# Two column groups of the embedding's gate as a seven-product pair, with sums of the third norm's activation

## The chip, the cores and the metric

The kernel runs on one core of a Trainium2 chip. A core has a matrix engine (TensorE, PE in the profile; PEld is its weight load), VectorE (DVE), ScalarE (ACT), GpSimd (POOL) and SyncE (SP), which issues most of the DMA transfers. Each engine works through its own queue in order and waits for the others by semaphores. The metric is the device time of one execution in microseconds; lower is better.

## The reference, cut to what matters

One layer on 256 rows of 2048 channels in float32: a feed-forward part, a mixer, a second feed-forward part, each with a layer norm behind it, and last the per-layer embedding, which is what the change touches:

```python
x = _layer_norm(ALPHA * x + 0.5 * _swiglu(x, ffn2_w1[i], ffn2_w3[i], ffn2_w2[i]), ln3_g[i], ln3_b[i])
x = x + jax.nn.sigmoid(x @ w_ple_gate[i]) * (p[i] @ w_ple_proj[i])
```

The gate is a product of 256x2048 by 2048x2048, the projection one of 256x256 by 256x2048. `_layer_norm` here is the third norm.

## The kernel before, in words

**Products.** Every float32 product is made of three matmuls in a rounded float32 format (fp32r in the profile): operand a is held as a high part and a low part, and hi x hi, hi x lo and lo x hi are summed (lines 1319 to 1321). A weight tile (`raw`) has 256 rows by 512 columns, seen as 128 partitions x 1024. It is split once: ScalarE casts the high part (L1264), VectorE subtracts it for the low part (L1268). An activation is held transposed in `ActT` tiles, high and low part alike, one for each chunk of 512 channels and each half of 128 rows. A `Unit` is one weight tile against one row half: 6 matmuls of 128x512.

**Groups.** `group` makes the plain product for 512 columns: 8 weight tiles, each used by two units, one for each row half (t = 0, 1). When a row half is complete, `done` reads the sum from PSUM.

**Seven products.** `seven` computes two column groups together by a Strassen-like scheme: over 4 chunks i of 512 channels it makes 7 units M1, M5, M7, M6, M3 and later M4, M2, where 8 plain units would stand for the same block. It needs sums of weights: M6 and M4 are made by VectorE (`plus`, L366); M5 and M7 either by VectorE or, where the chunk is in `loaded`, by a load that GpSimd issues and that adds to what is in the tile (`plus_load`, L372). It also needs sums of the activation, the `forms`: `form_turn` (L305) makes four sums of 128x256 on VectorE (L310 to L314) from the whole, unsplit activation (`act.whole`) and then splits them (L287 on ScalarE, L288 on VectorE). `both7` turns the seven products into two column groups (its `done`: copies on ScalarE, sums on VectorE, L420 and L426). `in_line` lays the units of such pairs in line, `weave` mixes them evenly into the plain units, by columns. The feed-forward parts and the mixer run this way; the embedding did not.

**Order.** The whole order is written out while the program is built. `program` is a list of units; a walk over it emits each unit's matmuls, then runs the work that is due (`Sched`, a clock in estimated microseconds with a heap of delayed turns), then emits further splits and loads. `HELD` limits by mode how many raw tiles and split pairs may be held at once; in the mode that rules the embedding before, (11, 6). `PAGES` is the pool of 51 pages that raw tiles, splits, activations and residuals share. `DELAY["form"]` and 5.0 set when the form turn of a chunk is due. What is emitted is fixed: at run time each engine follows its queue.

**The norm and the end.** `Norm.finish` normalizes, `Norm.turn` transposes a chunk (L519), applies scale and shift on ScalarE (L243, four 128x128 pieces), and splits (L287, L288); `Norm.affine` (L546, L547) later does the same to the residual on VectorE, two operations of 128x512 for each row half and chunk. The third norm turned its activation into tiles without forms. Then come four groups of the projection (L1168 copies them out) and four groups of the gate. `ple_done` takes a sigmoid (L243), multiplies by the projection (L1180), adds the residual (L1181) and stores (L1182). The last two tiles of the last group are `skewed`: both tiles for row half 0, then both for row half 1, and that group is finished in halves of 256 columns.

Of the kernel before, what the change touches and what calls it, by code (L numbers as in the profile page):

```python
# [10 lines left out]
ACT = mybir.ActivationFunctionType  # L11
ALU = mybir.AluOpType

P = 128
S = 256
TT = S // P
D = 2048
# [6 lines left out]
COL = 512  # L24
# [2 lines left out]
TEMP_BUFS = 6  # L27


HELD = {"ffn": (11, 6), "mix": (6, 6), "woven": (9, 6), "wide": (11, 6)}  # L30
RAW_EDGE, SPLIT_EDGE = 4, 11
EDGE = 6

AHEAD = 3
PSUM_BUFS = 8
SKEW = 6

HEAD = 20

# [15 lines left out]
DELAY = {  # L55
    "alpha": 24.0, "away": 5.0, "sig": 5.0, "form": 18.0, "ln_turn": 3.6, "ln_step": 2.1, "gb": 14.0, "h": 8.0, "silu": 6.0, "late": 9.0, "last": 5.0, "rest": 1.2, "mt": 3.2,
    "sbt": 4.6, "g0": 3.0, "g1": 4.0, "g2": 12.0, "cv0": 1.0, "cv1": 5.0, "cv2": 1.3,
    "m0": 4.0, "m1": 4.0, "m2": 2.0, "m3": 4.6, "m4": 4.6, "sa": 1.4, "s0": 6.5, "s1": 8.5, "s2": 3.0, "s3": 5.0, "s4": 5.5,
}
# [47 lines left out]
class ActT:  # L107


    def __init__(self, alloc, forms=None, later=False):  # L110
        self.alloc, self.soon = alloc, forms is not None and not later
        self.forms, self.whole = forms, {}
        self.tiles = {}
        self.left = {}

    def get(self, c, tt):
        if (c, tt) not in self.tiles:
# [48 lines left out]
def weave(main, side):  # L166

    n = sum(u.cols for u in main if isinstance(u, Unit))
    out, at, seen = [], 0, 0
    for u in main:  # L170
        out.append(u)
        if isinstance(u, Unit):
            seen += u.cols
            while at < len(side) and at * n < seen * len(side):
                out.append(side[at])
                at += 1
    return out
# [11 lines left out]
def kernel(  # L189
# [6 lines left out]
    nc = tc.nc  # L196
# [15 lines left out]
    def temp():  # L212
        sched.until(lambda: temps[0] < TEMP_BUFS)
        temps[0] += 1
        return temp_pool.tile([P, COL], F32, name="temp", tag="temp")

    def drop(n=1):
        temps[0] -= n
# [22 lines left out]
    def activate(out, in_, func, **kw):  # L241
        use_table(func)
        nc.scalar.activation(out, in_, func, **kw)  # L243
# [13 lines left out]
    def xres(t, c0, n=COL):  # L257
        return res[t, c0 // 1024][:, c0 % 1024:c0 % 1024 + n]
# [31 lines left out]
    def transposed(src, act, c, t):  # L290
        ps = misc([P, 4, P])
        for k in range(4):
            nc.tensor.transpose(ps[:, k], src[:, k * P:(k + 1) * P], ident[:])  # L293
        dst = act.get(c, t)
        nc.scalar.copy(dst[:, 0], ps[:])  # L295
        if act.soon:
            if c not in act.whole:
                act.whole[c] = big()
            nc.scalar.copy(act.whole[c][:, t * COL:(t + 1) * COL], ps.rearrange("q k s -> q (k s)"))  # L299
        nc.vector.tensor_tensor(out=dst[:, 1], in0=ps[:], in1=dst[:, 0], op=ALU.subtract)  # L300
        act.mark(c, t, 4)
        if act.soon and all(act.ready(c, h) for h in range(TT)):
            sched.spawn(form_turn(act, c), DELAY["form"] + 5.0 * c)

    def form_turn(act, c):  # L305

        a = [act.whole[c][:, t * COL:(t + 1) * COL] for t in range(TT)]
        s12, s34 = temp(), temp()
        l, r = slice(0, 2 * P), slice(2 * P, 4 * P)
        nc.vector.tensor_tensor(out=s12[:, l], in0=a[1][:, r], in1=a[1][:, l], op=ALU.subtract)  # L310
        nc.vector.scalar_tensor_tensor(out=s12[:, r], in0=s12[:, l], scalar=-1.0, in1=a[0][:, l],  # L311
                                       op0=ALU.mult, op1=ALU.subtract)
        nc.vector.tensor_tensor(out=s34[:, l], in0=a[0][:, l], in1=a[1][:, l], op=ALU.subtract)
        nc.vector.tensor_tensor(out=s34[:, r], in0=a[0][:, r], in1=s12[:, r], op=ALU.add)  # L314
        yield 4.0
        for h, src in enumerate((s12, s34)):
            dst = act.forms.get(c, h)
            split_psum(dst[:, 0], dst[:, 1], src.rearrange("q (k s) -> q k s", s=P))
            drop()
            act.forms.mark(c, h, 4)  # L320
# [18 lines left out]
    def group(w, rows, col0, cols, act, done):  # L339

        accs = [{} for _ in range(TT)]
        pairs = []
        for i, r in enumerate(rows):
            tile = plain(rows_of(w, r, col0, cols))
            pairs.append([Unit(tile, t, accs[t], act, r // COL, r % COL // P,
                               i == 0, i == len(rows) - 1, done) for t in range(TT)])
        return pairs
# [110 lines left out]
    def mode(name):  # L458
        program.append(Mode(name))
# [6 lines left out]
    class Norm:  # L466
# [33 lines left out]
        def finish(self, t):  # L500
            mv = small.tile([P, 2], F32, name="mv", tag="mv")
            nc.vector.bn_aggr(out=mv[:], in_=self.stats[t][:])  # L502
            rstd = small.tile([P, 1], F32, name="rstd", tag="rstd")
            activate(rstd[:], mv[:, 1:2], ACT.Sqrt, bias=eps[:, 0:1])
            nc.vector.reciprocal(out=rstd[:], in_=rstd[:])
            for c in range(4):
                xs = xres(t, c * COL)
                nc.vector.tensor_scalar(out=xs, in0=xs, scalar1=mv[:, 0:1], scalar2=rstd[:, 0:1],
                                        op0=ALU.subtract, op1=ALU.mult)
                sched.spawn(self.turn(t, c), DELAY["ln_turn"] + DELAY["ln_step"] * c)  # L510
            return
            yield

        def turn(self, t, c):

            xs, act = xres(t, c * COL), self.act
            ps = misc([P, 4, P])
            for k in range(4):
                nc.tensor.transpose(ps[:, k], xs[:, k * P:(k + 1) * P], ident[:])  # L519
            if act.soon:  # L520
                if c not in act.whole:
                    act.whole[c] = big()
                whole = act.whole[c][:, t * COL:(t + 1) * COL]
            else:
                whole = temp()[:]
            whole = whole.rearrange("q (k s) -> q k s", s=P)
            for k in range(4):
                i = 4 * c + k
                activate(whole[:, k], ps[:, k], ACT.Identity, scale=self.gb[:, i:i + 1], bias=self.gb[:, 16 + i:17 + i])
            dst = act.get(c, t)  # L530
            split_psum(dst[:, 0], dst[:, 1], whole)
            act.mark(c, t, 4)
            if not act.soon:
                drop()
            elif all(act.ready(c, h) for h in range(TT)):
                sched.spawn(form_turn(act, c), DELAY["form"] + 5.0 * c)
            sched.spawn(self.affine(t, c), self.wait[0] + self.wait[1] * (2 * c + t))
            return
            yield
# [596 lines left out]
    boundary("ffn")  # L1136


    x3T = ActT(act_tile)
    norm3 = Norm(ln3_g[0], ln3_b[0], x3T, None, (16.0, 4.0))  # L1140
    ffn(ffn2_w1[0], ffn2_w3[0], ffn2_w2[0], x2T, norm3)

# [21 lines left out]
    def proj_done(g):  # L1164
# [3 lines left out]
            nc.scalar.copy(proj[g // 2, t][:, (g % 2) * COL:(g % 2 + 1) * COL], ps)  # L1168
        return done

    def ple_done(g, n):

        def done(ps, t):
            sched.until(lambda: (t, g) in norm3.whole)
            ys = [temp()[:, :n] for _ in range(COL // n)]
            for k, y in enumerate(ys):
                activate(y, ps[:, k * n:(k + 1) * n], ACT.Sigmoid)
            for k, y in enumerate(ys):
                c0 = g * COL + k * n
                nc.vector.tensor_tensor(out=y, in0=y, in1=proj[c0 // 1024, t][:, c0 % 1024:c0 % 1024 + n], op=ALU.mult)  # L1180
                nc.vector.tensor_tensor(out=y, in0=y, in1=xres(t, c0, n), op=ALU.add)  # L1181
                nc.sync.dma_start(out=out[t * P:(t + 1) * P, c0:c0 + n], in_=y)  # L1182
                drop()
        return done

    at = len(program) - 24
    program.insert(at, load_p)
    for g in range(4):
        program.extend(flat(group(w_ple_proj[0], range(0, PLE, 2 * P), g * COL, COL, pT, proj_done(g))))
    for g, n in enumerate((COL, COL, COL, COL // 2)):  # L1190
        pairs = group(w_ple_gate[0], range(0, D, 2 * P), g * COL, COL, x3T, ple_done(g, n))
        program.extend(flat(pairs) if n == COL else flat(pairs[:-2]) + skewed(pairs[-2:]))


    def warm(n):
# [161 lines left out]
```

## Time and profile before

| | us |
|---|---|
| median of 3 runs | 2167.06 (2166.25 to 2169.68) |
| the profiled execution, its own time | 2169.55 |
| its span, first to last instruction | 2167.7 |
| TensorE busy | 2157.4 |
| VectorE busy | 1893.7 |
| ScalarE busy | 1347.1 |
| GpSimd busy | 218.2 |

The granted TensorE clock is 1.00 throughout. How to read the rows further down: a row of the timeline has the start and the duration in us, the engine, the line, the operation, output and inputs with their shapes, and how many were merged (x4); what stands in brackets is the engine's idle time before it and what ended that. The durations of neighbouring instructions overlap a little, so distances between starts tell what a full queue takes. A row of the stretches has the stretch, its length, the busy time (and count) of PE, PEld, DVE, ACT and POOL, the granted clock, the DMA's busy share and its GB/s. A row of waits has who waited for whom: us in total, times, the longest. A row of DMA issues ends in the median us from issue to landing.

### The profile page before, as it was taken

How to read it: one execution, taken by the hardware profiler on the slowest of the kernel's cores; microseconds unless marked ns; L12 is line 12 of the kernel's file. 1: busy time of each engine (PE TensorE's matmuls, PEld its weight loads, DVE VectorE, ACT ScalarE, POOL GpSimd, SP SyncE). 2: the span in 40 equal slices, each digit the busy share in tenths (PEclk: the TensorE clock that was granted, in tenths of full speed). 3: DMA queues.
4: the chain of work that ended last, by engine and by line, in shares of the span. 5: the costliest groups of instructions: out<-in, count | busy, mean ns of one | idle time of the engine just before them, and what ended most of it. 6: DMA issues, size and time to landing. Idle time of an engine off the chain costs nothing.

```text
span 2167.7 us, 27662 instructions
## 1 busy us (share of the span) xinstructions
PE 2157.4 (100%) x9798; PEld 1783.9 (82%) x9798; DVE 1893.7 (87%) x2088; ACT 1347.1 (62%) x1658; POOL 218.2 (10%) x186
## 2 busy tenths in 40 slices
PE   9999999999999999999999999999999999999999
PEld 7888888888888888888888888888888888888887
DVE  6899999999998898887878975799999999999974
ACT  7656666656655765677866554556556656656572
POOL 0111111111100000101010000011111111111000
PEclk9999999999999999999999999999999999999999
DMA  9899899999994667978898976679989999999642
GB/s 349 215 275 270 249 270 275 272 280 268 266 318 140 215 218 219 242 218 203 260 272 260 273 260 203 201 192 279 267 245 276 279 266 277 257 276 294 237 166 87
DMA packets 283179, 535.98 MB, mean 247 GB/s; under 512 B 17144, under 2 KB 34464, under 8 KB 283040
## 3 DMA queue, kind: packets, MB, share of 16 engines
q1 hardware_dynamic: 234624, 440.87, 59.9%
q0 software_dynamic: 48416, 93.33, 23.9%
q8 instruction: 77, 1.26, 0.2%
q14 instruction: 62, 0.51, 0.1%
HBM read 527.85 MB, written 6.29 MB: 246 GB/s over the span
## 4 chain that ended last, share of the span: by engine, by line
PE 93%; issue 2%; DMA 2%; DVE 2%; ACT 0%; POOL 0%; SPq 0%; POOLq 0%; DVEq 0%; ACTq 0%
PE mm L1319 30%; PE mm L1321 30%; PE mm L1320 30%; DMA raw<-in_ffn_w_dram 2%; PE ms L293 1%; DVE split L1268 1%; PE ms L519 0%; DVE raw L366 0%; PE ms L984 0%; PE ms L906 0%; PE ms L921 0%; PE ms L997 0%; POOL raw L372 0%; PE ms L1008 0%; DMA actT<-ymaway 0%
## 5 line engine op out<-in xcount | busy, mean ns | idle before, releaser
L1264 ACT CAST split<-raw 128x1024 fp32r<-128x1024 f32 (+1 forms) x1089 | 1089.4, 1044 | 513.8 <-DMA raw<-in_ffn_w_dram 172.7
L1268 DVE TENSOR_TENSOR split<-raw,split 128x1024 fp32r<-128x1024 f32 (+1 forms) x1089 | 1277.8, 1212 | 141.5 <-ACT split L1264 134.6
L1319 PE MATMUL mm<-split,actT 128*128 128x512 f32 x3064 | 1203.0, 393 | 1.2 <-DVE big L420 1.2
L1321 PE MATMUL mm<-split,actT 128*128 128x512 f32 x3064 | 1189.5, 388 | 0.6 <-DVE actT L300 0.6
L1320 PE MATMUL mm<-split,actT 128*128 128x512 f32 x3064 | 1188.4, 388 | 1.0 <-DVE split L1268 1.0
L1321 PEld LDWEIGHTS mm<-split,actT 128*128 128x128 f32 x3064 | 575.8, 188 | 120.7 <-DVE actT L300 1.4
L1320 PEld LDWEIGHTS mm<-split,actT 128*128 128x128 f32 x3064 | 576.6, 188 | 115.9 <-DVE split L1268 3.4
L1319 PEld LDWEIGHTS mm<-split,actT 128*128 128x128 f32 x3064 | 576.3, 188 | 115.5 <-issue 2.6
L372 POOL DMA_DIRECT2D raw<-in_ffn_w_dram x140 | 169.7, 1441 | 1204.9 <-DVE split L1268 809.6
L366 DVE TENSOR_TENSOR raw<-raw 128x1024 f32<-128x1024 f32 x190 | 231.6, 1220 | 1.6
L372 POOL DMA_DIRECT2D raw<-in_w_in_dram x38 | 46.0, 1426 | 505.7 <-DVE split L1268 432.5
L295 ACT CAST actT<-ms 128x512 fp32r<-128x512 f32 x60 | 35.1, 586 | 77.7 <-PE ms L293 73.2
L644 DVE SCALAR_TENSOR_TENSOR big<-mm,big 128x512 f32<-128x512 f32 x112 | 76.5, 685 | 2.9 <-PE mm L1321 2.8
L592 DVE TENSOR_TENSOR temp<-mm,temp 128x512 f32<-128x512 f32 x108 | 73.1, 686 | 1.8 <-PE mm L1321 0.6
L300 DVE TENSOR_TENSOR actT<-ms,actT 128x512 fp32r<-128x512 f32 x60 | 41.1, 687 | 16.5 <-ACT big L299 11.0
L243 ACT ACTIVATE temp<-mm 128x512 f32<-128x512 f32 (+1 forms) x36 | 20.3, 570 | 49.5 <-PE mm L1321 49.5
L239 ACT ACT_TABLE_LOAD x34 | 43.6, 1283 | 0.6
L288 DVE TENSOR_TENSOR actT<-temp,actT 128x512 fp32r<-128x512 f32 x40 | 26.5, 689 | 17.3 <-ACT actT L287 17.2
L1180 DVE TENSOR_TENSOR temp<-temp,big 128x512 f32<-128x512 f32 (+1 forms) x10 | 5.8, 583 | 26.4 <-ACT temp L243 26.4
L287 ACT CAST actT<-temp 128x512 fp32r<-128x512 f32 x40 | 23.9, 620 | 8.0 <-DVE temp L311 7.4
L243 ACT ACTIVATE rstd<-mv,eps 128x1 f32<-128x1 f32 x6 | 1.8, 295 | 41.8 <-DVE mv L502 41.8
L1123 DVE SCALAR_TENSOR_TENSOR big<-big,mm 128x512 f32<-128x512 f32 x8 | 5.5, 686 | 25.3 <-PE mm L1321 25.3
(133 smaller groups left out, 605.6 us busy)
## 6 DMA issues: line engine op xcount, KB each, us to landing
raw<-in_ffn_w_dram SPq DMA_DIRECT2D x527, 512.0 KB, 6.9
raw<-in_w_in_dram SPq DMA_DIRECT2D x144, 512.0 KB, 5.3
raw<-in_ffn_w_dram POOLq DMA_DIRECT2D x140, 512.0 KB, 9.8
raw<-in_w_in_dram POOLq DMA_DIRECT2D x38, 512.0 KB, 9.0
raw<-in_w_out_dram SPq DMA_DIRECT2D x32, 512.0 KB, 5.5
raw<-in_w_ple_gate_dram SPq DMA_DIRECT2D x32, 512.0 KB, 5.2
raw<-in_w_in_dram SPq DMA_DIRECT2D x56, 256.0 KB, 3.8
raw<-in_w_up_m_dram SPq DMA_DIRECT2D x16, 512.0 KB, 6.8
```

Source lines behind the costliest of these rows:

```text
L239: nc.scalar.preload_act_table_set(table[0])
L295: nc.scalar.copy(dst[:, 0], ps[:])
L300: nc.vector.tensor_tensor(out=dst[:, 1], in0=ps[:], in1=dst[:, 0], op=ALU.subtract)
L366: nc.vector.tensor_tensor(out=out.tile[:, :, :cols], in0=a.tile[:, :, :cols], in1=b.tile[:, :, :cols], op=ALU.add)
L372: nc.gpsimd.dma_start(out=out.tile[:, :, :cols], in_=src, accum_op=ALU.add)
L592: nc.vector.tensor_tensor(out=out, in0=a, in1=b, op=op)
L644: nc.vector.scalar_tensor_tensor(out=xs, in0=ps, scalar=0.5, in1=xs, op0=ALU.mult, op1=ALU.add)
L1264: nc.scalar.copy(hi[:, ks], r[:, ks])
L1268: nc.vector.tensor_tensor(out=lo[:, ks], in0=r[:, ks], in1=hi[:, ks], op=ALU.subtract)
L1319: nc.tensor.matmul(ps, hi, w[0][:, k, :u.cols], start=first, stop=False, skip_group_check=u.onto)
L1320: nc.tensor.matmul(ps, hi, w[1][:, k, :u.cols], start=False, stop=False, skip_group_check=u.onto)
L1321: nc.tensor.matmul(ps, lo, w[0][:, k, :u.cols], start=False, stop=last, skip_group_check=u.onto)
```

## The change

Column groups 1 and 2 of the gate become one seven-product pair (`both7` with accumulating loads in all four chunks), woven between groups 0 and 3, which stay plain. The first 4 units of group 0 go ahead of the weave, and the skewed last tiles of group 3 behind it. The third norm's activation gets forms, 8 further tiles and 4 whole chunks, with form turns due 6.0 + 3.0 c after a chunk is ready. The embedding's stage gets a mode of its own, (9, 6). `finish` is the old second half of `ple_done`; `ple_dest` and `ple_ready` give `both7` a temporary for each of the four blocks and finish it with sigmoid, product, residual and store.

```diff
-HELD = {"ffn": (11, 6), "mix": (6, 6), "woven": (9, 6), "wide": (11, 6)}
+HELD = {"ffn": (11, 6), "mix": (6, 6), "woven": (9, 6), "wide": (11, 6), "ple": (9, 6)}
+PLE_HEAD, PLE_FORM = 4, (6.0, 3.0)
@@ class ActT
+        self.gaps = DELAY["form"], 5.0
@@ transposed, Norm.turn
-            sched.spawn(form_turn(act, c), DELAY["form"] + 5.0 * c)
+            sched.spawn(form_turn(act, c), act.gaps[0] + act.gaps[1] * c)
@@
-    x3T = ActT(act_tile)
+    x3T = ActT(act_tile, ActT(act_tile))
+    x3T.gaps = PLE_FORM
     norm3 = Norm(ln3_g[0], ln3_b[0], x3T, None, (16.0, 4.0))
@@
+    def finish(ys, t, c0, n):
+        for k, y in enumerate(ys):
+            at = c0 + k * n
+            nc.vector.tensor_tensor(out=y, in0=y, in1=proj[at // 1024, t][:, at % 1024:at % 1024 + n], op=ALU.mult)
+            nc.vector.tensor_tensor(out=y, in0=y, in1=xres(t, at, n), op=ALU.add)
+            nc.sync.dma_start(out=out[t * P:(t + 1) * P, at:at + n], in_=y)
+            drop()
@@
+    gates7 = {}
+
+    def ple_dest(k, t):
+        gates7[k, t] = temp()
+        return gates7[k, t][:]
+
+    def ple_ready(k, t):
+        y = gates7[k, t][:]
+        activate(y, y, ACT.Sigmoid)
+        sched.until(lambda: (t, k + 1) in norm3.whole)
+        finish([y], t, (k + 1) * COL, COL)
@@
+    mode("ple")
     for g in range(4):
         program.extend(flat(group(w_ple_proj[0], range(0, PLE, 2 * P), g * COL, COL, pT, proj_done(g))))
-    for g, n in enumerate((COL, COL, COL, COL // 2)):
-        pairs = group(w_ple_gate[0], range(0, D, 2 * P), g * COL, COL, x3T, ple_done(g, n))
-        program.extend(flat(pairs) if n == COL else flat(pairs[:-2]) + skewed(pairs[-2:]))
+    first, last = (group(w_ple_gate[0], range(0, D, 2 * P), g * COL, COL, x3T, ple_done(g, n))
+                   for g, n in ((0, COL), (3, COL // 2)))
+    main = flat(first) + flat(last[:-2])
+    side = in_line([both7(w_ple_gate[0], COL, 2 * COL, x3T, ple_dest, ple_ready, every)])
+    program.extend(main[:PLE_HEAD] + weave(main[PLE_HEAD:], side) + skewed(last[-2:]))
```

More of the change, by code (lines that the diff above doesn't have):

```diff
@@ L535, in turn @@
             elif all(act.ready(c, h) for h in range(TT)):
-                sched.spawn(form_turn(act, c), DELAY["form"] + 5.0 * c)
+                sched.spawn(form_turn(act, c), act.gaps[0] + act.gaps[1] * c)
             sched.spawn(self.affine(t, c), self.wait[0] + self.wait[1] * (2 * c + t))
@@ L1177, in done @@
                 activate(y, ps[:, k * n:(k + 1) * n], ACT.Sigmoid)
[L1178 to L1183, printed above, removed]
-        return done
+            finish(ys, t, g * COL, n)
+        return done
+    gates7 = {}
[7 more added lines that the diff above has]
+        finish([y], t, (k + 1) * COL, COL)
     at = len(program) - 24
     program.insert(at, load_p)
+    mode("ple")
     for g in range(4):
         program.extend(flat(group(w_ple_proj[0], range(0, PLE, 2 * P), g * COL, COL, pT, proj_done(g))))
-    for g, n in enumerate((COL, COL, COL, COL // 2)):
-        pairs = group(w_ple_gate[0], range(0, D, 2 * P), g * COL, COL, x3T, ple_done(g, n))
-        program.extend(flat(pairs) if n == COL else flat(pairs[:-2]) + skewed(pairs[-2:]))
+    first, last = (group(w_ple_gate[0], range(0, D, 2 * P), g * COL, COL, x3T, ple_done(g, n))
[3 more added lines that the diff above has]
+    program.extend(main[:PLE_HEAD] + weave(main[PLE_HEAD:], side) + skewed(last[-2:]))
     def warm(n):
```

## The prediction

> **What bounds the kernel now.** I read the page first (busy shares, then the chain that ended last), then TensorE's waits, then the busy time of the last stage cut where the change begins.
>
> ```profile
> PE 2157.4 (100%) x9798; PEld 1783.9 (82%) x9798; DVE 1893.7 (87%) x2088; ACT 1347.1 (62%) x1658; POOL 218.2 (10%) x186
> PE 93%; issue 2%; DMA 2%; DVE 2%; ACT 0%; POOL 0%; SPq 0%; POOLq 0%; DVEq 0%; ACTq 0%
> PE mm L1319 <- DVE big L420: 1.2, 1, 1.2
> PE mm L1320 <- DVE split L1268: 0.7, 1, 0.7
> ...
> 2053.00:2075.40 22.40, 22.40 (x116) 18.55 (x115) 15.57 (x27) 15.72 (x35) 0.00 (x0) 1.00 0.34 115
> 2075.40:2085.40 10.00, 10.00 (x46) 8.27 (x45) 4.53 (x5) 9.90 (x22) 0.00 (x0) 1.00 0.52 168
> 2085.40:2162.50 77.10, 77.10 (x341) 63.67 (x339) 50.72 (x59) 30.59 (x35) 0.00 (x0) 1.00 0.35 124
> ```
>
> TensorE is 93% of the chain, its longest wait for another engine in the whole run is 1.2 us, and it never pauses in the last 110 us. VectorE (the third pair of numbers of a stretch) is the next engine: 87% overall, but 50.72 of 77.10 us in the last stretch, so it has 26 us free there. ScalarE is full from 2075.4 to 2085.4 (9.90 of 10), on the third norm.
>
> The end is set by the matmuls:
>
> ```profile
> 2075.63 0.40 PE L1320 MATMUL mm<-split,actT 128*128 128x512 f32 x1
> 2162.27 0.39 PE L1321 MATMUL mm<-split,actT 128*128 128x512 f32 x1
> 2162.69 0.66 ACT L243 ACTIVATE temp<-mm 128x256 f32<-128x256 f32 x2 [2.06 <-PE mm L1321]
> 2164.36 0.42 DVE L1181 TENSOR_TENSOR temp<-temp,big 128x256 f32<-128x256 f32 x1
> ```
>
> The first row is the second matmul of the gate, the second the last matmul of all. In the order of the program 382 matmuls lie between, so one costs 86.64/382 = 0.2268 us. After it come two sigmoids, two products, two sums and a store, up to the span's 2167.7. The change leaves this ending as it is: the same skewed pair in the same two halves.
>
> **Removed.** Two groups of 8 tiles x 2 row halves x 6 matmuls are 192; seven products over 4 chunks are 28 units of 6, 168. The built program has 24 matmuls fewer: 24 x 0.2268 = **-5.4 us** if TensorE never waits.
>
> **Added to VectorE.** By the order of the built queues: 12 more weight splits (28 for 16), 8 weight sums (`plus` of M6 and M4), 4 form turns (4 sums of 256 columns, 2 low parts) and 6 recombinations. What one costs in a full queue is the distance from its start to the next one's:
>
> ```profile
> 2085.42 1.23 DVE L1268 TENSOR_TENSOR split<-raw,split 128x1024 fp32r<-128x1024 f32 x1 [0.26 <-ACT split L1264]
> 2086.56 0.69 DVE L546 TENSOR_TENSOR big<-big 128x512 f32<-128x512 f32 x1
> 2087.89 4.62 DVE L1268 TENSOR_TENSOR split<-raw,split 128x1024 fp32r<-128x1024 f32 x4
> 2092.43 0.68 DVE L546 TENSOR_TENSOR big<-big 128x512 f32<-128x512 f32 x1
> ...
> 1420.04 0.42 DVE L310 TENSOR_TENSOR temp<-big 128x256 f32<-128x256 f32 x1
> 1421.51 1.22 DVE L366 TENSOR_TENSOR raw<-raw 128x1024 f32<-128x1024 f32 x1
> 1422.64 1.22 DVE L1268 TENSOR_TENSOR split<-raw,split 128x1024 fp32r<-128x1024 f32 x1
> 1426.11 1.29 DVE L288 TENSOR_TENSOR actT<-temp,actT 128x512 fp32r<-128x512 f32 x2
> 1427.31 0.42 DVE L310 TENSOR_TENSOR temp<-big 128x256 f32<-128x256 f32 x1
> 1864.53 1.41 DVE L592 TENSOR_TENSOR temp<-mm,temp 128x512 f32<-128x512 f32 x2
> 1865.86 1.22 DVE L1268 TENSOR_TENSOR split<-raw,split 128x1024 fp32r<-128x1024 f32 x1
> ...
> 2139.57 0.60 ACT L243 ACTIVATE temp<-mm 128x512 f32<-128x512 f32 x1 [11.05 <-PE mm L1321]
> 2140.20 0.69 DVE L1180 TENSOR_TENSOR temp<-temp,big 128x512 f32<-128x512 f32 x1 [8.56 <-ACT temp L243]
> 2141.56 0.69 DVE L1180 TENSOR_TENSOR temp<-temp,big 128x512 f32<-128x512 f32 x1
> ```
>
> A split is (2092.43 - 2087.89)/4 = 1.135 us, a weight sum 1422.64 - 1421.51 = 1.13, an affine pair (L546, L547) 2087.89 - 2086.56 = 1.33, a form's four sums 1.47, its two low parts 1.20, a recombination 1.33/2 = 0.67, a finishing pair (L1180, L1181) 1.36, and a sigmoid that VectorE stands waiting for 2140.20 - 2139.57 = 0.63. Added: 12 x 1.135 + 8 x 1.13 + 4 x 2.67 + 6 x 0.67 = 37.3 us, against 26 us free. This is the point on which I decide: the change makes **VectorE the bound** of the last stretch.
>
> **Where it bites first.** Up to the last turn of the norm both queues of ScalarE and VectorE are as before, except that the first form's four sums fall into VectorE's idle time after 2082.5:
>
> ```profile
> 2083.81 0.62 ACT L287 CAST actT<-temp 128x512 fp32r<-128x512 f32 x1
> 2084.34 7.70 ACT L1264 CAST split<-raw 128x1024 fp32r<-128x1024 f32 x8
> 2084.46 0.69 DVE L288 TENSOR_TENSOR actT<-temp,actT 128x512 fp32r<-128x512 f32 x1 [1.85 <-ACT actT L287]
> ```
>
> So M5's split of chunk 0 starts on VectorE at 2085.42, where the split above stood. Behind it the new queue has an affine pair, M6's weight sum, a split, and only then the low part of the form: 1.135 + 1.33 + 1.13 + 1.135 + 0.6 = 5.3 us, ready at 2090.75. TensorE reaches the matmul that reads it (49 after the row at 2075.63) at 2086.74 and waits **4.0 us**.
>
> **How it grows.** TensorE goes at a fixed pace and cannot win time back, so its end is set by the latest of all lags (VectorE's time at an operand less TensorE's unhindered time there). I added the queue up from 2085.42. M7 of chunk 1: 2111.2 against 2101.5, 9.7 late. M4 of chunk 1: 2150.2 against 2136.9, 13.3 late. Right behind that split stand M3's, M5's, M6's and M7's recombination with two finished blocks: 5 recombinations, 2 finishing pairs, two sigmoids waited for, and a weight sum; then M2's split of chunk 1, and TensorE has two units (2.7 us) between. From 2085.42 to the end of that split the queue holds 38 splits and weight sums (43.1), 8 affine pairs (10.6), 4 pairs of low parts (4.8), 3 form sums (4.4), 4 finishing pairs (5.4), 5 recombinations (3.3) and the 2 sigmoids (1.3): 72.9 us, so 2158.3; TensorE would be there at 2075.63 + 282 x 0.2268 = 2139.6. **18.7 us late.** After it the last weight sum and eight splits are 10.2 us of VectorE for 17.2 of TensorE, and the lag stays.
>
> **Accumulating loads.** M5's and M7's weights are made by 8 loads that GpSimd issues and that add in flight, now also for chunk 0.
>
> ```profile
> 2075.40 1.22 DVE L1268 TENSOR_TENSOR split<-raw,split 128x1024 fp32r<-128x1024 f32 x1 [0.74 <-ACT split L1264]
> 1836.16 5.76 DVE L1268 TENSOR_TENSOR split<-raw,split 128x1024 fp32r<-128x1024 f32 x5
> 1842.29 2.42 POOL L372 DMA_DIRECT2D raw<-in_ffn_w_dram  x2 [8.00 <-DVE split L1268]
> DMA packets 3219, 6.24 MB, mean 156 GB/s; under 512 B 186, under 2 KB 186, under 8 KB 3216
> raw<-in_ffn_w_dram POOLq DMA_DIRECT2D x2, 512.0 KB, 6.9
> DMA packets 8059, 10.82 MB, mean 216 GB/s; under 512 B 481, under 2 KB 5093, under 8 KB 8057
> raw<-in_w_in_dram POOLq DMA_DIRECT2D x4, 512.0 KB, 7.8
> DMA to landing us min/median/max: 5.7/9.7/14.0
> ACT split L1264 <- DMA raw<-in_w_ple_gate_dram: 3.9, 4, 2.0
> ```
>
> M1's split of chunk 0 ends at 2076.6; GpSimd starts 0.4 us after such a split (1842.29 against 1841.92). Landing took 6.9 us in a stretch that moved 156 GB/s (1400 to 1440), 7.8 at 216 (900 to 950), 9.7 at the median of all. With 6.9 M5's cast at 2084.34 isn't held up; with 9.7 it is for 2.3. M7's load of chunk 3 is as tight (its split is due 8.5 us after its release, the cast takes 1.05): 0 or 2.1. I take 8.0, by the second row, as the stretch from 2075.4 moved 168 GB/s and gets these loads on top: 0.6 for the first, 0.9 for the other, **+1.5**, bounds 0 and 4.4. The plain loads may wait for pages, as 12 more of the 51 are held (8 forms, 4 `whole`): before, casts waited 3.9 us in all for gate weights. ScalarE has less work per split than VectorE and runs ahead, which hides it: 0, at most 3.9. Neither can gain anything, so no bound lies below 0.
>
> **Sum.** 18.7 - 5.4 + 1.5 = +14.8. On the profiled execution 2169.55 gives 2184.4; that execution stood 2.5 above the median, so on the median 2167.06 + 14.8 = **2181.9**.
>
> **A colder clock.** A wait of 5 us on TensorE has no row here; the start of the kernel shows slow matmuls all the same:
>
> ```profile
> 7.22 0.77 PE L1319 MATMUL mm<-split,actT 128*128 128x512 f32 x1
> 10.20 0.40 PE L1319 MATMUL mm<-split,actT 128*128 128x512 f32 x1
> 10.44 0.40 PE L1320 MATMUL mm<-split,actT 128*128 128x512 f32 x1
> ```
>
> Six matmuls took 2.98 us where six later take 1.36: 1.6 us lost. If the wait ahead of M2 does the same, nothing hides it: rival C. [...]
>
> **The rivals.**
> - A, faster: every split is there in time, and the 24 matmuls are won: 2161.6. For it: TensorE waited for nothing before, and the same seven-product weave already runs in the feed-forward parts. Against: 37 us more on 26 free. It decides if VectorE's queue from 2085.4 to M2's split takes under 54.2 us (2139.6 - 2085.4) and not 72.9.
> - B, only the first form is late, and the rest catches up: -5.4 + 4.0, 2165.7. Against: the lag can't shrink below 9.7 at chunk 1.
> - D, the block ahead of M2 costs nothing, as VectorE has a lead by then: the lag of M4's split stays the latest, 13.3 - 5.4 + 1.5 = +9.4, 2176.5. For it: six split pairs may be held ahead; against: VectorE is already late at that split.
> - C, the cold restart: 2181.9 + 1.6 = 2183.5. For it: the slow start; against: no wait over 1.2 us in this trace to show it.
> - E, loads land late: 18.7 - 5.4 + 4.4 gives 2184.8 with landings at 9.7, and 2188.7 if the plain loads' 3.9 comes on top. For it: 12 pages less; against: ScalarE's lead.
>
> **How the numbers follow.** Forecast 45%, C 20%, D 13%, E 11%, A 6%, B 5%. The likeliest is 2182. The range reaches from D less 2.5 for small misses in the queue's sum to E: 2174 to 2188, and leaves out A, B and the upper end of E. About 0.2% (4.3 us) can be told from no change: faster is A with a little more, 7%; the same is B, 5%; slower 88%.
>
> **What would show it.** Right: in the last 90 us VectorE 95% busy or more; TensorE's waits there some 19 us, all for low parts and splits of VectorE, the first about 4 us near 2086.7 on a form's low part, the longest about 5 us on M2's split; the last matmul near 2176. Wrong: TensorE unbroken and the last matmul at 2156.8 (A); waits on casts for GpSimd's loads above 5 us (E); matmuls 0.43 apart after a wait (C). What would upset the sum is a VectorE idle after 2086, as I add it up without gaps but the two sigmoids.

## The result, and the profile after

The changed kernel takes 2186.35 us (median of 4 runs, 2183.97 to 2188.41) against 2167.2 for the kernel before beside it (2166.25 to 2169.68): ratio 1.0085, 95% interval 1.0074 to 1.0097. It is 19.15 us slower. Its profiled execution took 2187.23, 17.7 more than the one of before that the prediction reads (2169.55).

The page of the changed kernel, busy time by engine and the shares of the chain that ended last:

```profile
PE 2160.9 (99%) x9774; PEld 1781.4 (82%) x9774; DVE 1930.9 (88%) x2138; ACT 1363.8 (62%) x1680; POOL 227.9 (10%) x194
PE 84%; DVE 6%; DMA 5%; issue 3%; ACT 1%; POOL 0%; SPq 0%; DVEq 0%; POOLq 0%; ACTq 0%
```

The 24 matmuls are gone (9798 to 9774). VectorE has 37.2 us more to do, as forecast (37.3), and stands in the chain with 6% instead of 2%.

TensorE's waits from 2050 us to the end, and the one wait of ScalarE for a gate weight (who waited for whom: us in total, times, the longest):

```profile
PE mm L1341 <- DVE split L1289: 7.3, 5, 2.3
PE mm L1342 <- DVE actT L290: 3.3, 1, 3.3
PE mm L1340 <- ACT split L1285: 1.6, 1, 1.6
PE mm L1340 <- ACT actT L289: 0.9, 1, 0.9
...
ACT split L1285 <- DMA raw<-in_w_ple_gate_dram: 1.0, 2, 0.7
```

Before, TensorE waited for nothing here. Now it waits 13.1 us, 10.6 of them for low parts that VectorE makes. The 1.6 us on a cast are VectorE's too: that cast (M2's) stands in ScalarE's queue behind a sigmoid, which waited 2.09 us for a recombination on VectorE (L422). The loads held ScalarE up for 1.0 us only.

Stretches of the changed kernel (length; busy time and count of PE, PEld, DVE, ACT, POOL; granted clock; DMA share; GB/s):

```profile
2075.40:2085.40 10.00, 10.00 (x48) 8.26 (x47) 5.58 (x9) 9.57 (x22) 4.86 (x4) 1.00 0.67 144
2085.40:2180.00 94.60, 81.48 (x320) 63.77 (x318) 87.10 (x106) 49.28 (x58) 4.83 (x4) 0.91 0.57 157
2086.00:2160.00 74.00, 60.88 (x241) 46.98 (x239) 71.47 (x88) 40.43 (x48) 4.83 (x4) 0.92 0.70 191
2092.00:2096.00 4.00, 4.00 (x10) 3.14 (x11) 3.97 (x7) 2.81 (x5) 0.00 (x0) 0.50 1.10 263
2137.50:2141.50 4.00, 3.93 (x10) 3.11 (x11) 4.00 (x5) 2.34 (x3) 0.00 (x0) 0.58 0.86 280
2160.00:2165.00 5.00, 5.00 (x12) 3.98 (x13) 5.00 (x5) 3.40 (x4) 0.00 (x0) 0.50 0.00 0
```

From 2075.4 to 2085.4 TensorE is full, as before. From 2086 to 2160 VectorE is busy for 71.47 of 74 us and is the bound. Three short stretches have a clock of 0.5 to 0.58, each right behind waits; the last of them, 2160 to 2165, is also behind the last wait of all.

The timeline of TensorE around these places (start, duration, and in brackets the idle time and what ended it):

```profile
2087.96 0.50 PE L1340 MATMUL mm<-split,actT 128*128 128x512 f32 x1 [0.86 <-ACT actT L289]
...
2091.96 0.80 PE L1342 MATMUL mm<-split,actT 128*128 128x512 f32 x1 [3.27 <-DVE actT L290]
...
2108.77 0.50 PE L1341 MATMUL mm<-split,actT 128*128 128x512 f32 x1 [0.72 <-DVE split L1289]
...
2112.25 0.50 PE L1341 MATMUL mm<-split,actT 128*128 128x512 f32 x1 [1.80 <-DVE split L1289]
...
2137.57 0.50 PE L1341 MATMUL mm<-split,actT 128*128 128x512 f32 x1 [1.94 <-DVE split L1289]
...
2157.21 0.50 PE L1340 MATMUL mm<-split,actT 128*128 128x512 f32 x1 [1.64 <-ACT split L1285]
2160.00 0.80 PE L1341 MATMUL mm<-split,actT 128*128 128x512 f32 x1 [2.28 <-DVE split L1289]
...
2161.02 0.63 PE L1340 MATMUL mm<-split,actT 128*128 128x512 f32 x1
2161.44 0.63 PE L1341 MATMUL mm<-split,actT 128*128 128x512 f32 x1
...
2179.93 0.39 PE L1342 MATMUL mm<-split,actT 128*128 128x512 f32 x1
```

The matmul at 2160.00 is the second of M2's chunk 1, the place where the prediction put the latest lag. Behind it matmuls start 0.42 us apart instead of 0.227. Not every pair of waits has such a spell behind it: after 0.72 and 1.80 us (2108.77 and 2112.25) the next matmuls start 0.23 apart.

And what VectorE did from the first form to that operand:

```profile
2086.48 1.23 DVE L1289 TENSOR_TENSOR split<-raw,split 128x1024 fp32r<-128x1024 f32 x1 [0.69 <-ACT split L1285]
...
2150.30 1.22 DVE L1289 TENSOR_TENSOR split<-raw,split 128x1024 fp32r<-128x1024 f32 x1
2151.43 0.69 DVE L422 TENSOR_TENSOR temp<-mm,temp 128x512 f32<-128x512 f32 x1
2152.15 0.69 DVE L428 SCALAR_TENSOR_TENSOR temp<-temp,mm 128x512 f32<-128x512 f32 x1
2153.54 0.69 DVE L1177 TENSOR_TENSOR temp<-temp,big 128x512 f32<-128x512 f32 x1 [0.70 <-ACT temp L245]
...
2157.59 1.22 DVE L368 TENSOR_TENSOR raw<-raw 128x1024 f32<-128x1024 f32 x1
2158.73 3.49 DVE L1289 TENSOR_TENSOR split<-raw,split 128x1024 fp32r<-128x1024 f32 x3
```

Recombinations, finishing products, two sigmoids that VectorE stands waiting for (0.70 each) and a weight sum lie between the split at 2150.30 and M2's at 2158.73. From M5's split of chunk 0 (2086.48) to the end of M2's (one of the three at 2158.73, so 1.14 later) VectorE's queue took 73.4 us. Its only idle time on the way is the 1.4 us for the two sigmoids; it waits for TensorE nowhere.

**The account.** The last root of the third norm, the step at which both kernels leave the common course, on ScalarE's timeline of the changed kernel:

```profile
2065.67 0.29 ACT L245 ACTIVATE rstd<-mv,eps 128x1 f32<-128x1 f32 x1 [2.38 <-DVE mv L504]
```

and in the trace of before:

```profile
2065.07 0.29 ACT L243 ACTIVATE rstd<-mv,eps 128x1 f32<-128x1 f32 x1 [2.39 <-DVE mv L502]
```

From it to the last matmul is 114.26 us now and was 97.20: +17.06. The pieces: 24 matmuls, -5.44. M2's second matmul stands 94.33 us behind the root, and with a TensorE that never waits it would be there after 74.52 (282 x 0.2268 behind before's 2075.63): +19.81. From there to the last matmul are 76 steps, which took 19.93 us and would take 17.24: +2.69 for the slow clock. Sum +17.06. The two executions were already 0.60 apart at the root, which makes 17.66. The other 1.5 up to the 19.15 of the medians is how far each profiled execution lies above its median: 2.35 before, 0.88 now.

### The profile page after: what moved, and what is told of

It reads as the page before. It is cut to its first block, busy times and chain, and to the rows that moved or that the text cites. A ratio compares the mean times of both kernels' runs of the same rounds, so it can differ in the third digit from the quotient of the medians.

```text
span 2185.5 us, 27730 instructions
## 1 busy us (share of the span) xinstructions
PE 2160.9 (99%) x9774; PEld 1781.4 (82%) x9774; DVE 1930.9 (88%) x2138; ACT 1363.8 (62%) x1680; POOL 227.9 (10%) x194
## 4 chain that ended last, share of the span: by engine, by line
PE 84%; DVE 6%; DMA 5%; issue 3%; ACT 1%; POOL 0%; SPq 0%; DVEq 0%; POOLq 0%; ACTq 0%
PE mm L1341 27%; PE mm L1340 27%; PE mm L1342 27%; DMA raw<-in_ffn_w_dram 4%; DVE split L1289 3%; PE ms L295 1%; DVE raw L368 1%; DMA raw<-in_w_ple_gate_dram 0%; ACT split L1285 0%; PE ms L521 0%; DVE temp L594 0%; POOL raw L374 0%; PE ms L986 0%; DVE big L646 0%; PE ms L908 0%
## 5 line engine op out<-in xcount | busy, mean ns | idle before, releaser
L1285 ACT CAST split<-raw 128x1024 fp32r<-128x1024 f32 (+1 forms) x1101 | 1100.6, 1044 | 545.0 <-DVE raw L368 195.6
L1289 DVE TENSOR_TENSOR split<-raw,split 128x1024 fp32r<-128x1024 f32 (+1 forms) x1101 | 1291.4, 1211 | 145.9 <-ACT split L1285 137.9
L1341 PEld LDWEIGHTS mm<-split,actT 128*128 128x128 f32 x3056 | 576.0, 188 | 128.1 <-DVE split L1289 15.2
L368 DVE TENSOR_TENSOR raw<-raw 128x1024 f32<-128x1024 f32 x198 | 241.2, 1219 | 1.6
L245 ACT ACTIVATE temp<-temp 128x512 f32<-128x512 f32 (+1 forms) x38 | 22.4, 590 | 12.7 <-DVE temp L422 7.7
L245 ACT ACTIVATE big<-ms,gbT 128x128 f32<-128x128 f32 x64 | 24.1, 460 | 5.6 <-PE ms L521 5.6
```

What stands on the lines that cost most here:

```text
L368: nc.vector.tensor_tensor(out=out.tile[:, :, :cols], in0=a.tile[:, :, :cols], in1=b.tile[:, :, :cols], op=ALU.add)
L1285: nc.scalar.copy(hi[:, ks], r[:, ks])
L1289: nc.vector.tensor_tensor(out=lo[:, ks], in0=r[:, ks], in1=hi[:, ks], op=ALU.subtract)
L1341: nc.tensor.matmul(ps, hi, w[1][:, k, :u.cols], start=False, stop=False, skip_group_check=u.onto)
```

## Experiments

As kernels drift by a few us ahead of the norm from run to run (the last root starts between 2062.22 in head16 and 2065.67 in the changed kernel), the last column gives the distance from the last root of the norm to the last matmul of the profiled execution. The median of before, run beside each batch, is in brackets.

| kernel | median us (before) | ratio, 95% | root to last matmul |
|---|---|---|---|
| before | | | 97.2 |
| changed | 2186.35 (2167.2) | 1.0085, 1.0074 to 1.0097 | 114.3 |
| forms_only | 2168.53 (2166.62) | 1.0008, 0.9999 to 1.0018 | 97.9 |
| no_sums | 2174.9 (2166.62) | 1.0039, 1.0024 to 1.0054 | 104.9 |
| z_six_more | 2189.01 (2166.62) | 1.0099, 1.0084 to 1.0114 | 118.0 |
| head16 | 2187.17 (2166.62) | 1.0094, 1.0078 to 1.0111 | 117.3 |
| fill | 2185.62 (2166.84) | 1.0086, 1.0071 to 1.0101 | 115.4 |
| fill21 | 2182.14 (2167.51) | 1.0066, 1.0049 to 1.0083 | 111.8 |
| affine_early | 2179.18 (2167.51) | 1.0053, 1.0038 to 1.0068 | 107.1 |
| affine_pool | 2191.91 (2166.84) | 1.0115, 1.01 to 1.013 | 120.8 |
| affine_finish_pool | 2191.42 (2166.84) | 1.0113, 1.0098 to 1.0128 | 120.4 |
| pool_head16 | 2193.97 (2166.84) | 1.0125, 1.0108 to 1.0142 | 123.3 |
| rebalanced | 2197.8 (2167.51) | 1.014, 1.0125 to 1.0155 | 124.2 |
| sums_out_early | 2180.49 (2168.76) | 1.0057, 1.0044 to 1.0071 | 108.9 |

In the last two the root itself comes over 1 us late, as ScalarE waits 4.11 and 3.66 us for it instead of 2.38, so that their distance looks that much shorter.

### The forms alone

```diff
-    mode("ple")
...
-    program.extend(main[:PLE_HEAD] + weave(main[PLE_HEAD:], side) + skewed(last[-2:]))
+    for g, n in enumerate((COL, COL, COL, COL // 2)):
+        pairs = group(w_ple_gate[0], range(0, D, 2 * P), g * COL, COL, x3T, ple_done(g, n))
+        program.extend(flat(pairs) if n == COL else flat(pairs[:-2]) + skewed(pairs[-2:]))
```

The forms of the activation are still made, but all four groups are plain again, under the mode of before.

> The third norm's activation keeps its forms (8 tiles, 4 whole chunks, the changed form turns), but all four column groups of the gate are plain again. VectorE theory: 10.7 us of form work more on 26 us that were free in the last stretch; by the queue's sum no operand is over 0.5 us late, so 0 to +1.5 us on the kernel before, about 2168 us. Rival (the forms at the norm are what costs): +4 us or more, 2171 or above, with the wait on a form's work at the gate's start still there.

Measured: 2168.53, and a root-to-end distance 0.7 above before's. The last stretch:

```profile
2085.40:2165.00 79.60, 75.38 (x332) 61.76 (x330) 59.23 (x81) 33.80 (x42) 0.00 (x0) 0.99 0.42 139
```

VectorE has 59.23 us of work in 79.6, and TensorE waits 0.5 us for it, once, as expected: the forms' work is hidden. Casts wait 12.1 us for gate weights (3.9 before) without holding TensorE up. Making the sums of the activation isn't what costs; the pair is.

### VectorE's queue made shorter and longer

no_sums leaves out the eight weight sums of M6 and M4:

```diff
             def make():
+                if wa is w_gate:
+                    return
                 nc.vector.tensor_tensor(...
```

> Leaves out the 8 weight sums of M6 and M4 that VectorE makes for the pair, so these products use unsummed weights. VectorE theory: the queue ahead of M2's split of chunk 1 is 7 x 1.135 = 7.9 us shorter, it comes 10.7 us late in place of 18.8: 8 us faster than the changed kernel, about 2178, or 2175.5 if the cold spell behind that wait goes too. Rival (the accumulating loads, or TensorE itself, set the end): no change, 2186.

z_six_more repeats the one recombination ahead of M2's split (L428) six times:

```diff
-            nc.vector.scalar_tensor_tensor(out=z, in0=u, scalar=-1.0, in1=held[5],
...
+            for _ in range(7 if act is x3T else 1):
+                nc.vector.scalar_tensor_tensor(out=z, in0=u, scalar=-1.0, in1=held[5],
```

> Repeats one recombination of the pair (the subtraction that makes its block z) six times more on VectorE, to the same result. VectorE theory: 6 x 0.605 = 3.6 us more in front of M2's split, and all of it at the end: 3.6 us slower than the changed kernel, about 2190. Rival (loads or TensorE set the end): no change, 2186.

no_sums came to 2174.9: 11.5 less than the changed kernel, 9.4 by the distance from the root. M2's second matmul:

```profile
2148.88 0.50 PE L1344 MATMUL mm<-split,actT 128*128 128x512 f32 x1 [1.15 <-DVE split L1292]
```

Its root stands at 2063.01, 2.66 ahead of the changed kernel's, so this matmul comes 2160.00 - 2148.88 - 2.66 = 8.5 us earlier, for the 7 of the 8 sums that stand ahead of M2's split (7 x 1.135 = 7.9 us). The other 0.9 is a shorter slow spell behind it: from there to the last matmul it is 18.99 us and was 19.93. In z_six_more the seven operations on VectorE's timeline and the matmul that reads M2's split on TensorE's:

```profile
2150.13 5.02 DVE L429 SCALAR_TENSOR_TENSOR temp<-temp,mm 128x512 f32<-128x512 f32 x7
```

```profile
2162.30 0.80 PE L1342 MATMUL mm<-split,actT 128*128 128x512 f32 x1 [1.99 <-DVE split L1290]
```

Its root starts at 2063.71, 1.96 ahead of the changed kernel's, so the matmul is 2162.30 + 1.96 - 2160.00 = 4.3 us later, for 5.02 - 0.69 = 4.3 us of extra work: one for one. The distance from the root rose by 3.8, the median by 2.7, with intervals that overlap, so that here the trace decides. Work taken from the queue or put into it moves the end: VectorE is the bound up to M2's split.

### Is the first late form what costs?

```diff
-PLE_HEAD, PLE_FORM = 4, (6.0, 3.0)
+PLE_HEAD, PLE_FORM = 16, (6.0, 3.0)
```

> 16 units of the plain group go ahead of the weave in place of 4, so the pair starts 16 us later and its forms are ready long before. VectorE theory: the queue as a whole is as long as before, the first wait for a form goes, but the latest operand is still 17.9 us late: 1 us faster than the changed kernel, about 2185. Rival (the first wait for the form is what is lost, the rest follows from it): 4 us or more faster, 2182 or below.

Measured: 2187.17. The first wait for a form is gone, and the time isn't less. The waits of this kernel from 2050 on:

```profile
PE mm L1340 <- ACT split L1285: 7.8, 3, 4.2
PE mm L1341 <- DVE split L1289: 7.0, 10, 1.6
...
ACT split L1285 <- DMA raw<-in_w_ple_gate_dram: 17.4, 5, 8.5
```

TensorE waits 14.8 us in other places, and the end comes 3.0 us later by the root, where 1 us earlier was expected. The rival, that the first wait is all, falls. Something new shows, and the later end is put down to it, which no run here shows apart: ScalarE's casts waited 17.4 us for loads, 1.0 in the changed kernel. GpSimd issued the first accumulating loads at 2093.91 and not at 2077.84, for a reason that the last experiment gives.

### The slow clock behind the last wait

Dummy matmuls of 128x128 ahead of M2's unit of chunk 1 keep TensorE busy while it would wait: 36 in fill, 21 in fill21 (each shows as two instructions).

```diff
+    woven = main[:PLE_HEAD] + weave(main[PLE_HEAD:], side)
+    woven.insert(woven.index(side[-5]), lambda: warm(FILL))
```

> 36 dummy matmuls of 128x128 (some 4 us of TensorE) stand ahead of M2's unit of chunk 1, where TensorE waits for 4.4 us in all; nothing on VectorE changes. Cold-clock theory: the waits are filled, the twelve matmuls behind them go 0.23 us apart and not 0.43, and the 2.7 us go: about 2183.5 where the changed kernel has 2186.3. Rival (the slow matmuls have another cause, such as operands that come one by one): no gain, 2186 or a little more, and matmuls 0.43 apart remain there.

> As fill, with 21 dummy matmuls in place of 36: in that run the 36 took 8.2 us and pushed M2's unit some 3 us behind its split; 21 take 4.7 us and end before the split is there. Cold-clock theory: no matmul 0.43 apart behind them, and the 2.7 us are won: about 2183.6 where the changed kernel has 2186.3. Rival: no gain.

36 took 8.2 us, not 4, longer than the wait that they fill, and nothing was won (2185.62); yet the matmuls behind them start 0.23 apart, which speaks against the rival already. In fill21:

```profile
2153.46 4.85 PE L1222 MATMUL ms<-ones 128*128 128x128 f32 x42
2158.07 0.48 PE L1343 MATMUL mm<-split,actT 128*128 128x512 f32 x1
2158.38 0.40 PE L1344 MATMUL mm<-split,actT 128*128 128x512 f32 x1
2158.62 0.39 PE L1345 MATMUL mm<-split,actT 128*128 128x512 f32 x1
```

By the root (1.80 ahead of the changed kernel's) M2's second matmul comes at the same point, 0.2 later, but the next ones are 0.23 apart, and the distance from the root to the end is 2.5 us shorter. That is the 2.7 of the account, less those 0.2, with a granted clock of 1.00 from 2158 to 2163 where the changed kernel has 0.50 from 2160 to 2165: the cold clock is a cost of its own. The medians, 2182.14 and 2186.35, differ by more, but were taken beside different runs of before, and the intervals of their ratios overlap.

### The affine of the residual out of the way

```diff
-    norm3 = Norm(ln3_g[0], ln3_b[0], x3T, None, (16.0, 4.0))
+    norm3 = Norm(ln3_g[0], ln3_b[0], x3T, None, (1.0, 0.5))
```

This brings the affine pairs on VectorE forward, into idle time ahead of 2085.

> The changed kernel with the third norm's affine due 1.0 us after its turn (and 0.5 us more for each) in place of 16 and 4, on VectorE as before: most of its 8 pairs run in the gaps that VectorE has between the norm's turns, ahead of the overloaded stretch. VectorE theory: the latest operand is 10.8 us late in place of 18.8: 8 us faster than the changed kernel, about 2178, less 2.7 if the cold spell goes. Rival (the affine in the gaps delays the turns and so the forms by as much): 2184 or above.

Measured: 2179.18, 7.2 less than the changed kernel, and 7.2 by the root too. M2's second matmul on its timeline:

```profile
2152.74 0.50 PE L1341 MATMUL mm<-split,actT 128*128 128x512 f32 x1 [2.28 <-DVE split L1289]
```

With its root 1.05 ahead that is 6.2 us earlier than in the changed kernel, with waits of 0.61 and 2.28 us where there were 1.64 and 2.28; another 1.0 is a shorter slow spell behind it. That is near the 8 expected, and the rival's 2184 falls. Six of the eight affine pairs (8.0 us) moved ahead of M5's split of chunk 0, but that split itself came 1.3 us later, since its cast waited 1.70 us for a load where it had waited 0.34. It is the fastest of the versions here that keep the pair and leave nothing out, and still 0.53% slower than before.

### GpSimd takes over work of VectorE

```diff
-                nc.vector.tensor_tensor(out=xs, in0=xs, in1=self.g[c // 2][:, gs], op=ALU.mult)
...
+                eng = nc.gpsimd if self.act is x3T else nc.vector
+                eng.tensor_tensor(out=xs, in0=xs, in1=self.g[c // 2][:, gs], op=ALU.mult)
```

(and the same for the addition). affine_finish_pool also moves the product and the sum of `finish` for whole groups; pool_head16 adds the head of 16 to that.

> The third norm's affine (8 pairs of 128x512 operations, 10.6 us of VectorE) is done by GpSimd in the changed kernel. VectorE theory: the latest operand is 8.2 us late in place of 18.8, without a cold spell: about 2170. Rival (GpSimd's work slows VectorE, or its queue holds up the accumulating loads behind the affine): little gain, 2180 or above, with VectorE's operations longer than 1.22 us a split or casts waiting for loads.

> As affine_pool, and the products and sums that finish the 512-column blocks (6 pairs, 4 of them ahead of M2's split, where VectorE also stands waiting for two sigmoids) go to GpSimd too. VectorE theory: the latest operand is 5.7 us late (M7 of chunk 1): about 2167.5. Rival (GpSimd is late itself, its queue holds back loads or the last blocks): 2172 or above.

> As affine_finish_pool, with 16 units of the plain group ahead of the weave in place of 4. VectorE theory: no operand is over 0.7 us late, so nearly all of the 24 matmuls' 5.4 us is won: about 2162.5, faster than the kernel before by 0.2%. Rival (the forms still come late, or GpSimd holds up loads): 2167 or above.

All three missed by 22 to 31 us: they are slower than the changed kernel, though 16 operations and more have left VectorE. The rival that GpSimd slows VectorE has it. VectorE and GpSimd in affine_pool:

```profile
2101.04 2.12 DVE L312 TENSOR_TENSOR temp<-big 128x256 f32<-128x256 f32 x1
2101.11 1.77 POOL L549 TENSOR_TENSOR big<-big 128x512 f32<-128x512 f32 x1
...
2107.33 3.33 DVE L1290 TENSOR_TENSOR split<-raw,split 128x1024 fp32r<-128x1024 f32 x1
2107.85 1.72 POOL L549 TENSOR_TENSOR big<-big 128x512 f32<-128x512 f32 x1
```

A form's sum of 128x256 takes 2.12 us where it takes 0.42 alone, a split 3.33 instead of 1.22, each while GpSimd runs an operation of its own. The splits of this stage in affine_pool (minimum, median and maximum in ns):

```profile
L1290 DVE TENSOR_TENSOR split<-raw,split x42: 1212/1223/3331, 2069.6 to 2174.2; 128x1024 fp32r<-128x1024 f32 x42
```

TensorE's wait for them from 2050 us on:

```profile
PE mm L1342 <- DVE split L1290: 14.9, 6, 5.8
```

In the changed kernel none of these 42 took over 1.23 us, and TensorE waited 7.3 us for them. 0.42 and GpSimd's 1.77 make 2.19: VectorE's operation takes about as long as both one after the other. M5's split of chunk 0 and M2's of chunk 1 in the same trace:

```profile
2085.36 1.22 DVE L1290 TENSOR_TENSOR split<-raw,split 128x1024 fp32r<-128x1024 f32 x1
...
2163.98 3.49 DVE L1290 TENSOR_TENSOR split<-raw,split 128x1024 fp32r<-128x1024 f32 x3
```

From the first to the end of the other VectorE's queue takes 2163.98 + 1.14 - 2085.36 = 79.8 us. It took 73.4 with the affine's 10.6 in it, so without them 62.8 were due: what GpSimd relieves VectorE of costs it 17 us, more than it saves. In the second overlapping pair of rows the split's 3.33 us stand against 1.22 + 1.72 = 2.94, which is 0.39 short. By the rows VectorE's operation started first in both, by 0.07 and 0.52 us, and took the longer all the same; what makes it longer no run here shows. In pool_head16 casts also waited 27.8 us for accumulating loads, which stood in GpSimd's queue behind products that waited 33.9 us for sigmoids.

### Everything at once, and what the loads can bear

```diff
-HELD = {..., "ple": (9, 6)}
-PLE_HEAD, PLE_FORM = 4, (6.0, 3.0)
+HELD = {..., "ple": (7, 8)}
+PLE_HEAD, PLE_FORM = 24, (6.0, 3.0)
@@ seven
+            if wa is w_gate:
+                m4.make, m4.by_load = plus_load(b11, b21.src[0]), True
+                m6.soon.append(m4)
@@
-    norm3 = Norm(ln3_g[0], ln3_b[0], x3T, None, (16.0, 4.0))
+    norm3 = Norm(ln3_g[0], ln3_b[0], x3T, None, (0.2, 0.0))
```

> The pair with VectorE relieved: affine at once after its turn, M4's weight sums by accumulating loads, 24 plain units ahead of the weave, and 8 split pairs with 7 raw tiles held in place of 6 and 9. VectorE theory: no operand is late any more, and the 24 matmuls' 5.4 us are won: 2161.5, 0.25% faster than the kernel before. Rival (loads: with 7 raw tiles and 12 accumulating loads the casts wait for landings): 2167 or above, with ScalarE's waits on loads over 10 us.

It missed by 36 us and is the slowest of all. Its waits from 2050 on:

```profile
POOL raw L374 <- DVE split L1293: 179.8, 5, 131.4
ACT split L1289 <- DMA raw<-in_w_ple_gate_dram: 39.1, 5, 10.7
...
PE mm L1344 <- ACT split L1289: 19.9, 4, 7.5
PE mm L1345 <- DVE split L1293: 3.1, 5, 1.1
```

The place of VectorE is taken by the loads: casts wait 39.1 us for them, TensorE 19.9 for the casts, and 3.1 for VectorE. The first accumulating load is issued at 2103.76. Five edits went in together, so the last run takes the M4 loads and the tiles (7, 8) out again, leaves out the weight sums altogether as no_sums does, and keeps a head (12) and the affine at once:

```diff
-PLE_HEAD, PLE_FORM = 4, (6.0, 3.0)
+PLE_HEAD, PLE_FORM = 12, (6.0, 3.0)
@@ plus
+                if wa is w_gate:
+                    return
@@
-    norm3 = Norm(ln3_g[0], ln3_b[0], x3T, None, (16.0, 4.0))
+    norm3 = Norm(ln3_g[0], ln3_b[0], x3T, None, (0.2, 0.0))
```

> Leaves out the sixteen weight sums of M6 and M4 in the woven pair (eight tiles each in 128x512 columns, formed as eight 128x1024 operations), lets the third norm's affine come at once (0.2, 0.0 instead of 16.0, 4.0) and holds back the pair for 12 units instead of 4. No loads and no tiles are added; the matmuls are those of the changed kernel. Theory (VectorE's queue behind the end of the norm is what the pair waits for, and the loads keep up as long as none is added): with 8 x 1.2 us less in the queue, nothing of the affine behind the norm, and the first forms some 4 us later needed, the largest lag left is 2.5 us at M5's second operand, against 18.7 in the changed kernel; minus 5.4 us of matmuls that makes 2.9 us less than before, 2163.6, and with up to 4 us for waits in several pieces with a slow clock behind each, 2163 to 2168. Rival (a longer head and other orders make the casts wait for loads, as in the rebalanced version, where they waited 39 us): 2175 or more, with ScalarE's splits waiting 10 us or more for the gate's weights. Rival (the woven order itself costs TensorE time, whatever VectorE does): not under 2172.

2180.49: the theory's time is missed, and the rival of the loads has it (ScalarE's splits waited 19.9 us for gate weights). The other rival, that the woven order itself costs TensorE time, isn't excluded by the time; what speaks against it is that TensorE's waits have other causes, 8.1 us for casts and 5.0 for VectorE. With the same work for VectorE as in no_sums, much of it done earlier, it is 4.0 us slower by the root (5.6 in the medians, 2.1 of which lie between their runs of before, and the intervals overlap). The first accumulating loads on GpSimd, the cast that waits for one, and TensorE's wait for that cast, each from its engine's timeline:

```profile
2093.01 4.89 POOL L376 DMA_DIRECT2D raw<-in_w_ple_gate_dram  x4 [119.20 <-DVE split L1292]
...
2101.36 1.04 ACT L1288 CAST split<-raw 128x1024 fp32r<-128x1024 f32 x1 [9.14 <-DMA raw<-in_w_ple_gate_dram]
...
2102.45 0.80 PE L1343 MATMUL mm<-split,actT 128*128 128x512 f32 x1 [5.57 <-ACT split L1288]
```

In the changed kernel the first such load was issued at 2077.84:

```profile
2077.84 2.45 POOL L374 DMA_DIRECT2D raw<-in_w_ple_gate_dram  x2 [101.79 <-DMA raw<-in_w_ple_gate_dram]
```

M5's accumulating load adds to M1's tile, so it can't start ahead of M1's split. With a head of 4 that tile is the third of the program and its split is among the six pairs that may be held, made as the gate begins (2076.01 on VectorE); with a head of 12 it is the seventh, and its split comes at 2091.43. The load goes out 15.2 us later (2093.01 against 2077.84; 16.6 by the root), while M5 is needed only 8 units = 48 x 0.2268 = 10.9 us later. The head gives VectorE time and takes it from the loads. The affine at once costs a little too: it stands on VectorE ahead of the norm's statistics, so that ScalarE waits 3.66 us for them instead of 2.38. Which of these, and how much of what is left of VectorE's waits (5.0 us), would have to go for the pair to gain was not settled; no version here is faster than before.

## Why the prediction was right, and where its sum was off

- **24 matmuls, -5.4.** Right: 9774 are counted, and they run 0.227 apart where nothing holds them up.
- **VectorE becomes the bound.** Right, shown by three runs: forms_only (without the pair, no loss), no_sums (7.9 us less work ahead of M2's split, M2's matmul 8.5 earlier) and z_six_more (4.3 us more work, M2's matmul 4.3 later). The sign named for it was not met: 95% busy over 90 us was named, and it is 92% of the last 94.6 us. It is 97% up to M2's split; behind it VectorE has less than TensorE, as forecast.
- **The first wait, 4.0 us near 2086.7.** TensorE waited 0.86 and 3.27, 4.1 together, ending at 2091.96. It isn't what sets the end: VectorE's queue runs on through it, and a later lag covers it; without it, in head16, the end is no earlier.
- **M2's split, 18.7 late.** 19.8 measured. The queue took 73.4 us and not 72.9, and it began 0.46 late (M5's split at 2086.48, less 0.60 of drift, against 2085.42), for a load. "The longest wait about 5 us on M2's split" was 1.64 and 2.28 in two pieces, for cast and split; the longest single one was the first form's. The sum goes by lags, and needs neither. TensorE's waits add up to 13.1 us and not to "some 19". Of the other 6.7 us of the lag, 2.5 and 1.7 went into two earlier slow spells, which used up time that TensorE would have waited, and the rest lies around the waits. A, B (no lag at M2) and D (the block ahead of it costs nothing) fall by the same rows.
- **Accumulating loads, +1.5.** Only 0.46 us of it came, the late start of the queue just named: casts waited 1.0 us for gate weights in all, and the second of the two terms, M7's of chunk 3, isn't seen, though the loads took 9.3 us to land at the median and not 8.0. The figures of that second term don't fit each other: with the 0.4 us of GpSimd's start they are 0.95 for a landing of 8.0 and 2.65 for 9.7, without it 0.55 and 2.25, and the forecast has 0.9 and 2.1. E falls for this kernel; with a longer head it comes true.
- **The clock.** The forecast had no term for it, and C gave it 1.6: it came in with 2.7. This is the step that was mis-sized, and by its mechanism the outcome is C's, which had 20%. The price was taken from six matmuls at the start of the kernel, where the profile's clock column shows 1.00 although they start 0.42 to 0.69 us apart; here the slow spell behind the wait lasted 5.3 us and held twelve matmuls. fill21 shows it apart, 2.5 us. The two earlier spells (2092, 2137.5) added nothing to the end, since the next operand was late in any case.

With these sizes the sum is -5.44 + 19.81 (the 0.46 in it) + 2.69 = 17.1 in place of 14.8. The last matmul came at 2179.93 and not near 2176. The time, 2186.35, lies in the range but 4.4 us above the forecast: 2.3 of them by these terms, 0.6 by the drift ahead of the norm, and 1.5 because the profiled execution of before lay further above its median than that of the changed kernel. Those 1.5 and 0.6 are no part of the mechanism.

## What to carry to other kernels

A rewrite that trades matmuls for vector work is priced on the stage in which it runs: sum what VectorE must do up to each operand that TensorE needs, compare with TensorE's unhindered time there, and take the largest lag, not the sum of waits. Here the slow clock behind the last such wait counted on top (2.7 us), those behind earlier waits did not. Before work is moved to relieve the bound engine, ask whether work in the new place makes its operations longer (in affine_pool one of 0.42 us on VectorE lasted 2.12 while GpSimd ran one of 1.77) and which release it delays (M5's load waited for the split of M1's tile, to which it adds).

## What was not expected of the hardware

- **TensorE slowed down behind some short waits, but not behind all of them.** The clock fell to 0.58 in the stretch behind a wait of 1.94 us (2137.57; one of 0.52 stood 3.6 us ahead of it), and to 0.50 behind 1.64 and 2.28 with one matmul between. In such a spell matmuls start 0.42 us apart against 0.227. The first spell (0.50 from 2092 to 2096) follows a wait of 3.27; in no_sums one follows 0.98 and 1.15 with one matmul between (matmuls 0.42 to 0.43 apart from 2149.71 to 2152.70, a clock of 0.62 from 2150 to 2154). Waits of the same size also passed without a spell: 0.72 and 1.80 in the changed kernel (clock 1.00 from 2112 to 2116), and 1.24 and 1.15 with one matmul between in sums_out_early, where the next matmuls start 0.23 apart. What decides between them no run here shows.
- **Operations on VectorE took longer while GpSimd ran its own**, 2.12 us for one of 0.42 and 3.33 for one of 1.22; in affine_pool GpSimd's own rows of 128x512 lie between 1.32 and 2.28 us, where VectorE takes 0.69.
